# A hybrid mLSTM and sparse-attention trunk on one core: product lag in the attention backs, pieces of the gates' chain, and the order of the compression's weights

## The chip, the core and the metric

The kernel runs on one core of a Trainium2 chip. The metric is the device time of one execution in microseconds (us), as a median over several runs. Engines are named as in the profile: PE (TensorE matmuls), PEld (its weight loads), DVE (VectorE), ACT (ScalarE), POOL (GpSimd), SP (SyncE, which here only issues transfers).

## The reference

The model has 512 positions of width 1024 and two layers, each x += 1/2 SwiGLU, x += mixer, x += 1/2 SwiGLU, everything in float32. The first mixer is an mLSTM with 8 heads. The second is native sparse attention (NSA) with 16 query heads over 4 shared key/value heads, made once from the stream behind the first layer.

```python
log_i = ig + bif[0]; log_f = log_sigmoid(fg + bif[1])       # mLSTM gates
D = where(causal, b[t] - b[s] + log_i[s], -inf)             # b = cumsum(log_f)
h_out = (W @ v) / max(|den|, exp(-m));  W = exp(D - m) * (q @ k.T)
y = (rmsnorm(h_out, g_head) * sigmoid(og)) @ w_out
k_cmp = rmsnorm(silu((blocks(kc) + pe) @ w1) @ w2)          # compressed keys, v_cmp likewise
o = g_c * attn(q, k_cmp, v_cmp) + g_s * attn(q, k_sel, v_sel) + g_w * attn(q, k_win, v_win)
```

With 512 positions all eight blocks are selected and the window covers everything, so the selected and the window branch are both causal attention, each over its own keys and values.

## The kernel before

Activations lie transposed, features on partitions and the 512 positions along the free axis. Each float32 product is made of three float32r matmuls of a rounded high part and the remainder (`mm3`, L145): hi by hi, hi by lo, lo by hi. `split` (L151) makes the parts, the high one on ACT and the low one on DVE.

Weights come through one ring (`load_weight`, L102): SP issues a transfer of 512 KB into one of two `wraw` buffers, ACT rounds it into one of three `whi` and DVE makes `wlo`. The order of the weights is that in which the code asks for them, found in a dry pass, and a request loads up to two weights ahead.

The stages follow one another: ffn0, mlstm, ffn1, kv, ffn2, nsa, ffn3. In a stage Python generators write out the program order. `weave(main, fill, ratio)` takes one step of `main` and then on the average `ratio` steps of `fill`; a step of a projection is one `mm3`. Program order is not the order on an engine. The layer that places the instructions may put a later one first when it expects its operands sooner, with the earlier in program order preferred. An engine then works its own queue strictly in that order.

**mlstm (L311).** `project_qk(0)` takes eight steps, the row scale r is made, and `gates()` (L346) follows: a chain of about 25 operations on 8 partitions, most on DVE, with one exponential on ACT, to the running sums, the running maximum and its negative nM. All of it stands in one piece before the remaining 24 steps of `project_qk(0)`; the pair nM, the transposes of um and the columns uc and e2 stand behind 20 steps of `project_v(0)`. Later `heads(1)` is woven with `project_og(1)` and `project_out(0)` (64 steps, called rest) at 1.05, `finish(1)` (L517) with what is left at 4, and `project_out(1)` comes last. In `finish`, per head, a DVE operation scales num by a row that PE broadcasts, POOL multiplies by sig (L543), and `split` makes yhi and ylo, the operands of `project_out`.

**kv (L582)** makes the shared keys and values. `take` (L614) writes the unnormed keys and values A, with a shifted copy through POOL's DMA queue. `compress()` (L670) is returned as a generator and woven into ffn2, one step of it to 2.5 steps of ffn2 (L1000). Per kind (keys, values) and half it makes the operand F (A plus the block encoding, on POOL), splits it into Fh and Fl, waits three empty steps, and multiplies by two weights of c_w1, eight steps in all.

**nsa (L750).** A front per head makes scores S, row maxima on DVE, exponentials on ACT into pr, and the weighting by gate/z on POOL. A back per head (L880) has one PSUM accumulator po (one buffer for all heads): it starts with the product of the compressed weights ct (one buffer), and then works five groups. For each, PE transposes pieces of pr into one of two PSUM tiles pt, `split` makes pth and ptl (three buffers each), and the products of the group before are added to po, so products run one group behind. At the head's end ACT copies half of po and DVE adds the other into o. `compressed(b)` (L812) makes ct for a pair of heads; its last step waits until the back of head 2b-1 has begun, and the fronts of the pair stand behind it. `Steps` objects mix backs, fronts and fills (projections of later queries and half of the output) by the lines below, behind a start in which q1 takes four steps, then r, the gates, and the rest of q1 with fronts between.

```python
for _ in backs[h]:
    fill.steps(0.9)
    front.steps(2.5)
```

Of the kernel before, what the change touches and what calls it, by code (L numbers as in the profile page):

```python
# [10 lines left out]
F32 = mybir.dt.float32  # L11
F32R = mybir.dt.float32r
BF16 = mybir.dt.bfloat16
I32 = mybir.dt.int32
AF = mybir.ActivationFunctionType
ALU = mybir.AluOpType
# [29 lines left out]
def run(gen):  # L46
    for _ in gen:
        pass
# [42 lines left out]
class Net:  # L91
# [220 lines left out]
    def mlstm(self):  # L312
        nc, tc = self.nc, self.tc
        TT, STT, TS = nc.vector.tensor_tensor, nc.vector.scalar_tensor_tensor, nc.vector.tensor_scalar
        with ExitStack() as ctx:
# [32 lines left out]
            def gates():  # L348
                bif = self.g[:H, G_BIF:G_BIF + 2]
                li, f, t1, t2, t3 = (row(n, "big", BIG) for n in ("li", "f", "t1", "t2", "t3"))  # L350
                TT(li, pg[:H], r[:H], op=ALU.mult)
                TS(li, li, bif[:, 0:1], None, op0=ALU.add)
                TT(f, pg[32:32 + H], r[32:32 + H], op=ALU.mult)
                TS(f, f, bif[:, 1:2], None, op0=ALU.add)

                STT(t1, f, -1.0, f, op0=ALU.mult, op1=ALU.max)
                nc.scalar.activation(t1, t1, AF.Exp, scale=-1.0)
                TS(t2, t1, 2.0, None, op0=ALU.add)
                nc.vector.reciprocal(t3, t2)
                TT(t1, t1, t3, op=ALU.mult)  # L360
                TT(t2, t1, t1, op=ALU.mult)
                TS(t3, t2, 1.0 / 15.0, None, op0=ALU.mult)
                for c in (13.0, 11.0, 9.0, 7.0, 5.0, 3.0):
                    STT(t3, t3, 1.0 / c, t2, op0=ALU.add, op1=ALU.mult)
                STT(t3, t3, 1.0, t1, op0=ALU.add, op1=ALU.mult)
                TS(f, f, 0.0, None, op0=ALU.min)
                STT(f, t3, -2.0, f, op0=ALU.mult, op1=ALU.add)

                one = self.ones[:H, :1].to_broadcast([H, T])
                um = mp.tile([40, T], F32, name="um", tag="tmp", bufs=3)  # L370
                nc.gpsimd.memset(um, 0.0)
                nc.vector.tensor_tensor_scan(t1, one, f, 0.0, op0=ALU.mult, op1=ALU.add)
                TT(um[:H], li, t1, op=ALU.subtract)
                nc.vector.tensor_tensor_scan(t2, one, um[:H], 0.0, op0=ALU.mult, op1=ALU.max)
                TT(um[32:], t1, t2, op=ALU.add)
                TS(t2, t2, -1.0, None, op0=ALU.mult)
                yield
                nM = pair("nM", t2)
                up = ps_nm()[:, :160].rearrange("p (t c) -> p t c", t=NTB)
                for tb in range(NTB):  # L380
                    nc.tensor.transpose(up[:, tb, :], um[:, tb * P:(tb + 1) * P], self.ident[:40, :40])
                uc = mp.tile([P, NTB, H], F32, name="uc")
                nc.scalar.copy(uc, up[:, :, :H])
                e2 = mp.tile([P, NTB, H], F32, name="e2")
                nc.scalar.activation(e2, up[:, :, 32:], AF.Exp, scale=-2.0)
                yield nM, uc, e2
# [130 lines left out]
            def finish(half):  # L517
# [20 lines left out]
                for h in range(4 * half, 4 * half + 4):  # L538
                    pc = ps_nm()
                    self.mm(pc, pick(h), cr, True, True)  # L540
                    n = num[h]
                    STT(n, n, self.g[:, G_HEAD + h:G_HEAD + h + 1], pc, op0=ALU.mult, op1=ALU.mult)
                    nc.gpsimd.tensor_tensor(n, n, sig[h], op=ALU.mult)  # L543
                    hi = self.xp.tile([P, T], F32R, name="yhi", tag="xhi")
                    lo = self.xp.tile([P, T], F32R, name="ylo", tag="xlo")
                    self.split(n, hi, lo)
                    y[h] = (hi, lo)
                    yield
# [16 lines left out]
            g = gates()  # L565
            next(g)
            run(qk0)
            v0 = project_v(0)
            for _ in range(20):
                next(v0)  # L570
            nM, uc, e2 = next(g)
            run(v0)
# [11 lines left out]
            weave(heads(1), rest, 1.05)  # L584
            sigmoids(1)
            weave(finish(1), rest, 4)
# [4 lines left out]
    def kv(self):  # L591
# [17 lines left out]
        with ExitStack() as ctx:  # L609
            pp = ctx.enter_context(tc.tile_pool(name="kps", bufs=1, space=PSUM, reuse_waits="tile"))  # L610
            mp = ctx.enter_context(tc.tile_pool(name="ks", bufs=1, reuse_waits="tile"))
            ps_mm = lambda: pp.tile([P, T], F32, name="pmm", tag="mm", bufs=6)
            x, ssq = self.norm_in(G_KV)
            def take(b, ps):  # L614
                if b < 4:

                    for j in range(2):
                        t, s = A[b // 2][:, 2 * (b % 2) + j, :], slice(64 * j, 64 * j + 64)
                        TT(t[:64], ps[s], r[s], op=ALU.mult)
                        nc.gpsimd.dma_start(t[64:, :T - 1], t[:64, 1:])  # L620
                    return
                br = (b - 4) // 2
                sq = mp.tile([P, T], F32, name="ksq", tag="ksq", bufs=2)
                nc.scalar.activation(sq, ps, AF.Square)
                f = self.head_scale(mp, aux([P, NTB, 2]), sq, var, HD)
                fb = mp.tile([P, NTB, 2, HD], F32, name="kfb", tag="ksq", bufs=2)
                nc.scalar.activation(fb, f[:, :, :, None].to_broadcast([P, NTB, 2, HD]), AF.Copy, scale=HD ** 0.5)
                yield
                fp = aux([P, T])
                for tb in range(NTB):  # L630
                    self.mm(fp[:, tb * P:(tb + 1) * P], fb[:, tb].rearrange("p h d -> p (h d)"), self.ident, True, True)
                kn = mp.tile([P, T], F32, name="kn", tag="kn", bufs=2)
                nc.scalar.copy(kn, fp)
                STT(kn, ps, self.g[:, G_K + 1 + br:G_K + 2 + br], kn, op0=ALU.mult, op1=ALU.mult)
                for j in range(2):
                    K = self.K[2 * (b % 2) + j]
                    s, o = slice(64 * j, 64 * j + 64), slice(64 - 64 * j, 128 - 64 * j)
                    nc.scalar.activation(K[s, br, :], kn[s], AF.Copy)
                    TT(K[o, br, :], kn[s], K[s, br, :].bitcast(F32), op=ALU.subtract)

            held = []
            for b in range(8):
                w = self.weight("kv_t", b)
                ps = ps_mm()
                for k in range(KB):
                    self.mm3(ps, self.strip(w, k), x[k], k == 0, k == KB - 1)
                if b == 0:
                    rc, var = self.rstd_columns(ssq, aux([P, NTB]))
                if b == 1:
                    r = self.rstd_rows(rc, aux([P, T]))  # L650
                held.append(take(b, ps))
                if b > 0:
                    held = [t for t in held if next(t, t) is None]
            ps4 = [ps_mm() for _ in range(NTB)]
            for kp in range(4):
                w = self.weight("kv_v", kp)
                for tb in range(NTB):
                    for kk in range(2):
                        k = 2 * kp + kk
                        l = tuple(t[:, tb * P:(tb + 1) * P] for t in x[k])  # L660
                        self.mm3(ps4[tb], l, self.strip(w, kk), k == 0, k == KB - 1)
            for t in held:
                run(t)
            for tb in range(NTB):
                pv = ps4[tb].rearrange("p (h d) -> p h d", d=HD)
                V = self.V[tb]
                nc.scalar.activation(V[:, :, :HD], pv, AF.Copy, scale=rc[:, tb:tb + 1])
                STT(V[:, :, HD:], pv, rc[:, tb:tb + 1], V[:, :, :HD].bitcast(F32), op0=ALU.mult, op1=ALU.subtract)

        def compress():  # L670

            n = KVH * NCMP
            for kind in range(2):
                av = A[kind].rearrange("p h (c s) -> p s h c", s=16)
                hp = aux([P, 256])
                for half in range(2):
# [7 lines left out]
                    for _ in range(3):  # L684
                        yield
                    for j in range(2):
# [60 lines left out]
        return compress(), r  # L747


    def nsa(self):  # L750
        nc, tc = self.nc, self.tc
        TT, STT, TS = nc.vector.tensor_tensor, nc.vector.scalar_tensor_tensor, nc.vector.tensor_scalar
        with ExitStack() as ctx:
# [56 lines left out]
            def compressed(b):  # L810
# [25 lines left out]
                yield lambda: started[0] >= 2 * b  # L836
# [3 lines left out]
                t = cw[b] = mp.tile([P, T], F32R, name="ct", tag="ct", bufs=1)  # L840
# [4 lines left out]
            def head(h):  # L845
# [34 lines left out]
                def back():  # L880
# [3 lines left out]
                    held, left = None, [4, 4]  # L884
# [9 lines left out]
                    for group in groups:  # L894
# [10 lines left out]
                        if held:  # L905
                            apply(*held)
                        held = group, at, hi, lo
# [5 lines left out]
                    apply(*held)  # L913
# [52 lines left out]
            for _ in range(4):  # L966
                next(q1)
# [5 lines left out]
            for _ in q1:  # L973
                front.steps(1.2)
# [135 lines left out]
```

## Time and profile before

| | us |
|---|---|
| median of 3 runs (2060.71 to 2061.84) | 2061.43 |
| the profiled execution | 2058.35 |
| its span, first to last instruction | 2056.6 |
| PE busy in the span | 2024.7 |
| DVE, ACT, POOL busy | 1122.9, 817.0, 188.9 |

A wait is idle time of an engine before an instruction, put down to what ended it. A matmul's end is modelled, some 0.16 us behind the point at which the next one can start, so a PE wait as listed is a little shorter than what it costs.

### The profile page before, as it was taken

The page shows a single profiled execution, that of the slowest core. Times are in us where ns is not written, and L with a number is a line of the kernel's source. Part 1 is how long each engine was busy: PE and PEld are TensorE (multiplying, and loading weights), DVE is VectorE, ACT ScalarE, POOL GpSimd, SP SyncE. Part 2 cuts the span into 40 slices and gives each one's busy share as a digit, 9 for nine tenths or more (in the row PEclk, how much of TensorE's full clock was granted, in tenths as well). Part 3 has the DMA queues.
Part 4 walks back from the last instruction along what each step waited for, and adds up shares of the span by engine and source line. Part 5 has one row for each costly group of instructions (what it writes and reads, how often), then busy time and mean ns, then how long its engine had stood idle before and what let it go on. Part 6 is the DMA issues. An engine that isn't in the chain of part 4 may idle for free. (4 is left out here: it accounts for less than half of the span.)

```text
span 2056.6 us, 24443 instructions
## 1 busy us (share of the span) xinstructions
PE 2024.7 (98%) x9460; PEld 1662.0 (81%) x9460; DVE 1122.9 (55%) x1796; ACT 817.0 (40%) x1409; POOL 188.9 (9%) x235
## 2 busy tenths in 40 slices
PE   8999999999999999999999999999999999999999
PEld 6888888778878888888878888887777788888887
DVE  6434345777765444445656444445788874434443
ACT  5223233455643222223443322224888763223231
POOL 1000000012210000000101000001544420000000
PEclk9999999999999999999999999999999999999999
DMA  4232322323123322323333323333111113332332
GB/s 161 93 103 91 103 94 86 103 93 92 62 72 103 101 94 86 109 90 105 95 100 126 114 95 91 103 94 93 52 42 42 42 56 99 92 101 89 101 97 95
DMA packets 56468, 188.12 MB, mean 91 GB/s; under 512 B 6816, under 2 KB 7456, under 8 KB 56352
## 3 DMA queue, kind: packets, MB, share of 16 engines
q1 hardware_dynamic: 55392, 184.47, 28.8%
q8 instruction: 74, 1.21, 0.3%
q0 software_dynamic: 384, 1.05, 0.2%
q10 hardware_dynamic: 576, 1.05, 0.1%
q14 instruction: 42, 0.34, 0.1%
HBM read 177.10 MB, written 2.10 MB: 87 GB/s over the span
## 5 line engine op out<-in xcount | busy, mean ns | idle before, releaser
L124 ACT ACTIVATE whi<-wraw 128x1024 fp32r<-128x1024 f32 (+3 forms) x399 | 360.3, 916 | 989.5 <-PE pmm L143 813.3
L143 PE MATMUL pmm<-xhi,whi 128*128 128x512 f32 x1672 | 656.7, 393 | 7.6 <-ACT whi L124 7.6
L143 PE MATMUL pmm<-xhi,wlo 128*128 128x512 f32 x1672 | 653.6, 391 | 0.0
L143 PE MATMUL pmm<-xlo,whi 128*128 128x512 f32 x1672 | 653.0, 391 | 0.1
L125 DVE TENSOR_TENSOR wlo<-wraw,whi 128x1024 fp32r<-128x1024 f32 (+3 forms) x399 | 419.6, 1061 | 77.0 <-ACT whi L124 66.1
L143 PEld LDWEIGHTS pmm<-xhi,whi 128*128 128x128 f32 x1672 | 314.2, 188 | 70.4 <-ACT whi L124 8.8
L143 PEld LDWEIGHTS pmm<-xhi,wlo 128*128 128x128 f32 x1672 | 313.8, 188 | 66.9 <-DVE wlo L125 1.0
L143 PEld LDWEIGHTS pmm<-xlo,whi 128*128 128x128 f32 x1672 | 314.1, 188 | 62.4 <-DVE xlo L188 0.6
L143 PE MATMUL pmm<-ghi,whi 128*128 128x512 f32 x704 | 274.1, 389 | 0.0
L143 PE MATMUL pmm<-ghi,wlo 128*128 128x512 f32 x704 | 273.9, 389 | 0.0
L143 PE MATMUL pmm<-glo,whi 128*128 128x512 f32 x704 | 273.9, 389 | 0.0
L271 DVE TENSOR_TENSOR fu<-pmm,r 128x512 f32<-128x512 f32 x88 | 60.8, 691 | 259.0 <-PE pmm L143 258.9
L309 DVE SCALAR_TENSOR_TENSOR h<-pmm,h 128x512 f32<-128x512 f32 x96 | 66.1, 691 | 238.9 <-PE pmm L143 238.9
L269 DVE TENSOR_TENSOR ft<-pmm,r 128x512 f32<-128x512 f32 x88 | 60.8, 691 | 180.9 <-PE pmm L143 180.9
L143 PEld LDWEIGHTS pmm<-ghi,wlo 128*128 128x128 f32 x704 | 132.2, 188 | 27.6
L143 PEld LDWEIGHTS pmm<-ghi,whi 128*128 128x128 f32 x704 | 132.2, 188 | 27.3
L143 PEld LDWEIGHTS pmm<-glo,whi 128*128 128x128 f32 x704 | 132.2, 188 | 27.2
L198 POOL TENSOR_TENSOR ssq<-ssq,sq 128x512 f32<-128x512 f32 x18 | 28.0, 1556 | 999.6 <-ACT sq L197 999.6
L152 ACT ACTIVATE ghi<-ft 128x512 fp32r<-128x512 f32 x88 | 55.7, 633 | 79.1 <-DVE ft L272 79.1
L873 POOL TENSOR_SCALAR pr<-pr,rz,gate 128x512 f32<-128x512 f32 (+3 forms) x128 | 79.6, 631 | 77.8 <-DVE rz L869 68.3
L868 ACT ACTIVATE pr<-S,nx,c 128x512 f32<-128x512 f32 (+3 forms) x128 | 78.1, 617 | 0.9
L153 DVE TENSOR_TENSOR glo<-ft,ghi 128x512 fp32r<-128x512 f32 x88 | 60.4, 687 | 17.2 <-ACT ghi L152 17.1
(297 smaller groups left out, 2054.0 us busy)
## 6 DMA issues: line engine op xcount, KB each, us to landing
wraw<-in_ffn_in SPq DMA_DIRECT2D x176, 512.0 KB, 3.4
wraw<-in_ffn_out SPq DMA_DIRECT2D x64, 448.0 KB, 3.3
wraw<-in_ffn_out SPq DMA_DIRECT2D x32, 512.0 KB, 3.6
wraw<-in_m_qk SPq DMA_DIRECT2D x8, 512.0 KB, 3.4
wraw<-in_m_v SPq DMA_DIRECT2D x8, 512.0 KB, 3.5
wraw<-in_m_og SPq DMA_DIRECT2D x8, 512.0 KB, 3.4
wraw<-in_m_out SPq DMA_DIRECT2D x8, 512.0 KB, 3.4
wraw<-in_kv_t SPq DMA_DIRECT2D x8, 512.0 KB, 3.4
```

The lines of the kernel that those rows point to most:

```text
L124: nc.scalar.activation(hi[:p, c], raw[:p, c], AF.Copy)
L125: nc.vector.tensor_tensor(lo[:p, c], raw[:p, c], hi[:p, c].bitcast(F32), op=ALU.subtract)
L143: self.nc.tensor.matmul(out, lhsT, rhs, start=start, stop=stop)
L152: self.nc.scalar.activation(hi, src, AF.Copy)
L153: self.nc.vector.tensor_tensor(lo, src, hi.bitcast(F32), op=ALU.subtract)
L198: (nc.gpsimd if b < 4 else nc.vector).tensor_tensor(t, t, sq, op=ALU.add)
L269: nc.vector.tensor_tensor(t, pa, r, op=ALU.mult)
L271: nc.vector.tensor_tensor(u, pb, r, op=ALU.mult)
L309: nc.vector.scalar_tensor_tensor(h, po[j], 0.5, h, op0=ALU.mult, op1=ALU.add)
L868: nc.scalar.activation(s, S[:, i, :n], AF.Exp, bias=nx[:, i:i + 1], scale=cc, accum_out=z[:, i:i + 1])
L873: nc.gpsimd.tensor_scalar(s, s, rz[:, i:i + 1], gate[:, tb, gi:gi + 1], op0=ALU.mult, op1=ALU.mult)
```

## The change

The gates' chain yields eight times and is woven at 5 steps of qk and v to a piece, with nM, um's transposes, uc and e2 in the last piece. The multiply by sig goes to DVE in the second half. `heads(1)` takes 0.9 fill steps instead of 1.05, `finish(1)` 5 instead of 4. `compress()` starts before the `kv_v` projection: its first step (F, Fh and Fl of the keys' first half) stands there, one empty step follows instead of three, and elsewhere four stand in place of three; its first c_w1 weight comes before the first two of ffn2. In the attention, products run two groups behind, ct has two buffers and may be made one pair of heads earlier, and q1 takes all eight matmul steps before the row scale is made, with no front between.

```diff
 def gates():
     nc.scalar.activation(t1, t1, AF.Exp, scale=-1.0)
+    yield
...
+    yield
     for c in (13.0, 11.0, 9.0, 7.0, 5.0, 3.0):
         STT(t3, t3, 1.0 / c, t2, op0=ALU.add, op1=ALU.mult)
+        if c in (11.0, 7.0, 3.0):
+            yield
...
     yield
-    nM = pair("nM", t2)
+    gated.append(pair("nM", t2))
...
-    yield nM, uc, e2
+    gated.extend((uc, e2))
 def finish(half):
-    nc.gpsimd.tensor_tensor(n, n, sig[h], op=ALU.mult)
+    (nc.vector if half else nc.gpsimd).tensor_tensor(n, n, sig[h], op=ALU.mult)
...
-g = gates()
-next(g)
-run(qk0)
-v0 = project_v(0)
-for _ in range(20):
-    next(v0)
-nM, uc, e2 = next(g)
-run(v0)
+gated, rest = [], chain(qk0, project_v(0))
+weave(gates(), rest, 5)
+nM, uc, e2 = gated
+run(rest)
...
-weave(heads(1), rest, 1.05)
+weave(heads(1), rest, 0.9)
 sigmoids(1)
-weave(finish(1), rest, 4)
+weave(finish(1), rest, 5)
 def kv(self):
...
+    left = compress()
+    next(left)
     ps4 = [ps_mm() for _ in range(NTB)]
...
 def compress():
-    hp = aux([P, 256])
     for half in range(2):
...
-        for _ in range(3):
+        for _ in range(4 if half or kind else 1):
             yield
+        if half == 0:
+            hp = aux([P, 256])
...
-return compress(), r
+return left, r
 def nsa(self):
...
-    yield lambda: started[0] >= 2 * b
+    yield lambda: started[0] >= 2 * b - 2
-    t = cw[b] = mp.tile([P, T], F32R, name="ct", tag="ct", bufs=1)
+    t = cw[b] = mp.tile([P, T], F32R, name="ct", tag="ct", bufs=2)
...
-        if held:
-            apply(*held)
-        held = group, at, hi, lo
+        if len(held) == 2:
+            apply(*held.popleft())
+        held.append((group, at, hi, lo))
...
-    apply(*held)
+    while held:
+        apply(*held.popleft())
...
-for _ in range(4):
+for _ in range(KB):
     next(q1)
...
-for _ in q1:
-    front.steps(1.2)
+run(q1)
```

## Rows read from the trace of the kernel before

**Rows 1.** The page: busy time of the engines, and the commonest group of matmuls.

```profile
PE 2024.7 (98%) x9460; PEld 1662.0 (81%) x9460; DVE 1122.9 (55%) x1796; ACT 817.0 (40%) x1409; POOL 188.9 (9%) x235
...
L143 PE MATMUL pmm<-xhi,whi 128*128 128x512 f32 x1672 | 656.7, 393 | 7.6 <-ACT whi L124 7.6
```

**Rows 2.** Windows: stretch, its length, busy time of each engine, granted clock, DMA.

```profile
515.00:561.00 46.00, 45.91 (x218) 37.31 (x217) 38.93 (x68) 30.48 (x70) 11.24 (x12) 1.00 0.21 66
...
561.00:605.00 44.00, 39.31 (x170) 29.74 (x168) 31.55 (x57) 22.93 (x38) 10.07 (x7) 1.00 0.23 76
605.00:960.00 355.00, 355.00 (x1574) 294.18 (x1575) 161.24 (x201) 103.93 (x127) 4.55 (x3) 1.00 0.31 96
...
1424.00:1500.00 76.00, 71.74 (x422) 56.16 (x421) 53.44 (x150) 55.67 (x143) 33.22 (x46) 0.98 0.21 58
1500.00:1600.00 100.00, 95.86 (x599) 77.58 (x598) 81.39 (x215) 87.30 (x242) 50.31 (x74) 1.00 0.16 43
1600.00:1692.00 92.00, 90.65 (x510) 72.88 (x509) 71.95 (x144) 66.08 (x158) 31.38 (x45) 1.00 0.16 47
```

**Rows 3.** Waits of PE: who for whom, total us, times, longest us.

```profile
PE paux L143 <- ACT whi L124: 2.9, 2, 1.5
PE pmm L143 <- ACT yhi L152: 2.8, 2, 1.5
PE po L143 <- DVE ptl L153: 2.4, 3, 0.9
PE vps L143 <- DVE wlo L125: 1.7, 1, 1.7
PE po L143 <- DVE o L918: 1.4, 1, 1.4
PE pt L143 <- DVE rq L217: 1.4, 1, 1.4
PE po L143 <- ACT pth L152: 1.3, 5, 0.5
PE pt L900 <- DVE ct L153: 1.2, 2, 0.7
...
PE pmm L143 <- DVE ylo L153: 0.7, 1, 0.7
```

**Rows 4.** Timeline of the gates' chain: start, us, engine, line; then PE's first use.

```profile
391.08 3.34 DVE L359 RECIPROCAL t<-t 8x512 f32<-8x512 f32 x1
...
416.53 0.68 DVE L337 TENSOR_TENSOR nM<-t,nM 8x512 fp32r<-8x512 f32 x1 [0.16 <-ACT nM L336]
...
424.77 0.39 PE L143 MATMUL pnm<-nM,sel 128*128 128x512 f32 x1
```

**Rows 5.** Groups from 561 to 587 (finish of the second half), then the timeline of DVE.

```profile
L543 POOL TENSOR_TENSOR num<-num,sig 128x512 f32<-128x512 f32 x4 | 5.6, 1415 | 22.2 <-DVE num L542 22.2
...
L542 DVE SCALAR_TENSOR_TENSOR num<-num,gains,pnm 128x512 f32<-128x512 f32 x4 | 3.0, 738 | 0.7 <-PE pnm L143 0.7
...
577.43 1.61 DVE L153 TENSOR_TENSOR ylo<-num,yhi 128x512 fp32r<-128x512 f32 x1 [0.36 <-ACT yhi L152]
...
579.62 0.68 DVE L153 TENSOR_TENSOR ylo<-num,yhi 128x512 fp32r<-128x512 f32 x1
```

**Rows 6.** Timeline of POOL, SP (c_w1's issues) and PE around the end of kv.

```profile
985.91 2.39 POOL L679 TENSOR_TENSOR F<-A,gains 128x992 f32<-128x992 f32 x1
...
1032.44 0.33 SPq L117 DMA_DIRECT2D wraw<-in_c_w  x1
...
1056.62 0.33 SPq L117 DMA_DIRECT2D wraw<-in_c_w  x1
...
1062.50 0.38 PE L143 MATMUL paux<-whi,Fh 128*124 128x256 f32 x1 [1.55 <-ACT whi L124]
```

**Rows 7.** The longest wait of a product in NSA, and the window that follows it.

```profile
1485.59 0.50 PE L143 MATMUL po<-ct,VC 128*128 128x512 f32 x1 [1.43 <-DVE o L918]
...
1488.10:1491.40 3.30, 3.30 (x12) 2.84 (x11) 2.55 (x6) 1.06 (x1) 0.62 (x1) 0.50 0.00 0
```

More of the change, by code (lines that the diff above doesn't have):

```diff
@@ L367, in gates @@
                 STT(f, t3, -2.0, f, op0=ALU.mult, op1=ALU.add)
+                yield
                 one = self.ones[:H, :1].to_broadcast([H, T])
@@ L373, in gates @@
                 TT(um[:H], li, t1, op=ALU.subtract)
+                yield
                 nc.vector.tensor_tensor_scan(t2, one, um[:H], 0.0, op0=ALU.mult, op1=ALU.max)
@@ L608, in kv @@
         A = [lp.tile([P, KVH, T], F32, name=f"A{kind}") for kind in range(2)]
[L609 to L668, printed above, removed]
@@ L745, in compress, with take @@
             late.close()
-        return compress(), r
+        with ExitStack() as ctx:
+            pp = ctx.enter_context(tc.tile_pool(name="kps", bufs=1, space=PSUM, reuse_waits="tile"))
+            mp = ctx.enter_context(tc.tile_pool(name="ks", bufs=1, reuse_waits="tile"))
+            ps_mm = lambda: pp.tile([P, T], F32, name="pmm", tag="mm", bufs=6)
+            x, ssq = self.norm_in(G_KV)
+            def take(b, ps):
+                if b < 4:
+                    for j in range(2):
+                        t, s = A[b // 2][:, 2 * (b % 2) + j, :], slice(64 * j, 64 * j + 64)
+                        TT(t[:64], ps[s], r[s], op=ALU.mult)
+                        nc.gpsimd.dma_start(t[64:, :T - 1], t[:64, 1:])
+                    return
+                br = (b - 4) // 2
+                sq = mp.tile([P, T], F32, name="ksq", tag="ksq", bufs=2)
+                nc.scalar.activation(sq, ps, AF.Square)
+                f = self.head_scale(mp, aux([P, NTB, 2]), sq, var, HD)
+                fb = mp.tile([P, NTB, 2, HD], F32, name="kfb", tag="ksq", bufs=2)
+                nc.scalar.activation(fb, f[:, :, :, None].to_broadcast([P, NTB, 2, HD]), AF.Copy, scale=HD ** 0.5)
+                yield
+                fp = aux([P, T])
+                for tb in range(NTB):
+                    self.mm(fp[:, tb * P:(tb + 1) * P], fb[:, tb].rearrange("p h d -> p (h d)"), self.ident, True, True)
+                kn = mp.tile([P, T], F32, name="kn", tag="kn", bufs=2)
+                nc.scalar.copy(kn, fp)
+                STT(kn, ps, self.g[:, G_K + 1 + br:G_K + 2 + br], kn, op0=ALU.mult, op1=ALU.mult)
+                for j in range(2):
+                    K = self.K[2 * (b % 2) + j]
+                    s, o = slice(64 * j, 64 * j + 64), slice(64 - 64 * j, 128 - 64 * j)
+                    nc.scalar.activation(K[s, br, :], kn[s], AF.Copy)
+                    TT(K[o, br, :], kn[s], K[s, br, :].bitcast(F32), op=ALU.subtract)
+            held = []
+            for b in range(8):
+                w = self.weight("kv_t", b)
+                ps = ps_mm()
+                for k in range(KB):
+                    self.mm3(ps, self.strip(w, k), x[k], k == 0, k == KB - 1)
+                if b == 0:
+                    rc, var = self.rstd_columns(ssq, aux([P, NTB]))
+                if b == 1:
+                    r = self.rstd_rows(rc, aux([P, T]))
+                held.append(take(b, ps))
+                if b > 0:
+                    held = [t for t in held if next(t, t) is None]
+            left = compress()
+            next(left)
+            ps4 = [ps_mm() for _ in range(NTB)]
+            for kp in range(4):
+                w = self.weight("kv_v", kp)
+                for tb in range(NTB):
+                    for kk in range(2):
+                        k = 2 * kp + kk
+                        l = tuple(t[:, tb * P:(tb + 1) * P] for t in x[k])
+                        self.mm3(ps4[tb], l, self.strip(w, kk), k == 0, k == KB - 1)
+            for t in held:
+                run(t)
+            for tb in range(NTB):
+                pv = ps4[tb].rearrange("p (h d) -> p h d", d=HD)
+                V = self.V[tb]
+                nc.scalar.activation(V[:, :, :HD], pv, AF.Copy, scale=rc[:, tb:tb + 1])
+                STT(V[:, :, HD:], pv, rc[:, tb:tb + 1], V[:, :, :HD].bitcast(F32), op0=ALU.mult, op1=ALU.subtract)
@@ L883, in back @@
                     groups = (((0, 1), (0, 3)), ((0, 0),), ((0, 2), (1, 2)), ((1, 1), (1, 3)), ((1, 0),))
-                    held, left = None, [4, 4]
+                    held, left = deque(), [4, 4]
                     started[0] += 1
```

## The prediction

> **What bounds the kernel now.** I read the page first, for the busiest engine. PE is busy 2024.7 of 2056.6 us [rows 1], so only PE's gaps can be won; the other engines matter where they open one. The windows come next: they show where the gaps lie. From 605 to 960 us PE has none, and 1574 matmuls take 355 us, 0.2255 us each [rows 2]. So the large FFN stretches have nothing to give. From 561 to 605 PE misses 44 - 39.31 = 4.7 us, and in the three NSA windows 4.3 + 4.1 + 1.4 = 9.8 us [rows 2]. The list of PE's waits then says what ended each gap [rows 3]. The nine rows there add up to 15.8 us, and the change touches all nine. What they really cost is more, since a wait is counted from a matmul's modelled end: a matmul is listed with 0.393 us [rows 1] and the next starts after 0.2255, so each interruption costs about 0.16 us on top. Rows 3 hold 18 of them, 2.9 us. One gap has a sequel: after the 1.43 us wait at 1485.6 the granted clock is 0.50 for 3.3 us, which is the lower of the two levels, 1.2 GHz [rows 7]. Half of that time is lost, 1.7 us. Before the fall PE had that wait and a run of small score matmuls. All that the change can win by these rows is 15.8 + 2.9 + 1.7 = 20.4 us.
>
> **The change part by part.** The sum is made against the profiled execution, 2058.35 us (span 2056.6 and 1.75 around it); the median stands 3.1 us above it, and I add the same difference back.
>
> *Gates in pieces.* No operation is added or removed. Before, the whole chain stood ahead of the weights that come with the following steps, so on DVE's queue the weight split that PE needed came behind it; the longest single piece is a reciprocal of 3.34 us [rows 4]. PE stood 1.7 us for that split [rows 3]. In pieces, each weight split has its place ahead of the pieces written later. The chain itself then ends when? Its last piece stood behind 8 + 24 + 20 steps of qk and v, and now behind 8 + 8 x 5 = 48, so it is not due later. If it were, nM is complete at 417.2 and PE first uses it at 424.8 [rows 4], which covers 7.5 us. Gain 1.7 + 0.16 = 1.9 us; bounds from +0.5 (the reciprocal catches another split) to -1.9.
>
> *The end of mLSTM.* The steps left for `finish(1)` go from 64 - 47 = 17 to 64 - 40 = 24 (45 steps of `heads(1)` by 1.05 and by 0.9). Seven steps of three matmuls are 7 x 3 x 0.2255 = 4.7 us of PE work moved from the heads to the finish. Per head, DVE's scaling takes 0.74 us, POOL's multiply 1.42 on the average, and a low split 0.68, or 1.61 where it runs beside POOL [rows 5]. On DVE the multiply should be like the low split, 0.68 us: both read two 512-column operands of the same size. The chain per head gets about 0.7 us shorter and DVE's own part comes to 0.74 + 0.68 + 0.68 = 2.1 us per head. PE waited 2.8 + 0.7 us here [rows 3] in three gaps, 4.0 us in all. The new cover would hide most of it, but the work is taken from a stretch in which DVE is busy 38.9 of 46 us [rows 2]: with 4.7 us less of PE work in it DVE would need 38.9 of 41.3, less about a microsecond of weight splits that move along. There some of it comes back as PE waiting for DVE. I take 1.5 us of 4.0; bounds +1 to -4.
>
> The Trainium skill ("Perfetto Trace Analysis", Optimizing Scalar/DVE Operations) says that work moved between GpSimd and VectorE might not help, since they share an SBUF read port. By that rule the move gains nothing and the 1.5 us would be 0.8, from the cover alone (an estimate: half). The rows speak against it here, since the low split beside POOL loses 0.9 us, and with both operations on one engine there is nothing beside it.
>
> *kv into ffn2.* F was already made at 985.9 [rows 6], far ahead of its place in the program and 55 us before its use, so making it sooner is worth nothing. POOL's 2.39 us and the four transfers it issues stay where they are; the cost of the edit is 0, and if POOL were late the 55 us cover it. What matters is the weights' order: the first c_w1 transfer is issued at 1032.4 after two of ffn2 and now comes before them, and the second at 1056.6 is what PE waits for at 1062.5 [rows 6]. The two waits are 2.9 us [rows 3], 3.2 with the restarts. The first should go, but then ffn2's second weight comes one place later on SP, ACT and DVE, and its first matmuls alternate between two weights; some of it is given back. The second c_w1 weight still needs a buffer of the ring of three that the first one frees only after four steps. I take 1.7; bounds +1 to -3.2.
>
> *Start of NSA.* PE waits 1.4 us for the row scale [rows 3]. Four more steps of q1, 12 x 0.2255 = 2.7 us, now stand before it and cover it. The same 2.7 us are missing as filler beside the first fronts, where fills of q2 must stand in. Gain 1.6 less 0.7, 0.9; bounds +2 (all missing filler is idle, less 0.7) to -1.6.
>
> *Products two groups behind.* The same matmuls, transposes and splits. Products waited 1.3 + 2.4 us in eight gaps [rows 3], 3.7 + 8 x 0.16 = 5.0 us. One more group gives a split another round of fronts and fills before it is needed. ACT and DVE are busy 87.3 and 81.4 of 100 us in the middle window [rows 2], so they still run behind at times, and what is late next is a transpose that waits for one of two pt tiles. I take 2.8; bounds +8 to -5.0, the upper end from the second rival.
>
> *Compressed weights a pair ahead.* Transposes waited twice for ct's split, 1.2 us [rows 3], 1.5 with restarts. The split is still made once per pair and still holds a pt tile, but at a less loaded moment, and the even heads' fronts no longer stand behind it. I take half, 0.7; bounds +1.5 to -1.5.
>
> *The wait for o.* With its restart and the slow clock it cost 1.43 + 0.16 + 1.7 = 3.3 us, at one of 15 changes of head. The new order neither removes nor repeats it by design; I take half, 1.5; bounds +3.3 to -3.3.
>
> The sum: 1.9 + 1.5 + 1.7 + 0.9 + 2.8 + 0.7 + 1.5 = 11.0 us. 2058.35 - 11.0 = 2047.4, and by the median 2061.43 - 11.0 = **2050.4 us**.
>
> **The rivals.** *First, slower: the single accumulator.* Behind the last transposes of a head now stand the products of two groups instead of one, then ACT's copy and DVE's add, and the next head's first product needs the same po. If PE waits for that at most changes of head as it did once, 1.43 + 0.16 = 1.6 us [rows 7], it costs 1.6 each. The other terms without the wait for o are 9.5 us, so it decides from six changes on; at 12 of 15 it is 19.2 - 9.5 = 9.7 us slower, 2071. For it: one buffer for all heads. Against it: only one of 15 changes shows such a wait now, and the transposes of the next head are independent of po and can be placed before its first product. Chance 0.1.
>
> *Second, given back: two pt tiles.* The products no longer wait, but transposes run further ahead and wait for a pt tile, as they did twice for 0.6 us each [rows 3]. Once per head that is 16 x 0.6 = 9.6 us; the 11.0 us shrink to 1.4, and the time is 2060. For it: ACT at 87%. Against it: only two such waits now, and the number of transposes and splits is unchanged. A rule of the Trainium skill stands for this case ("Perfetto Trace Analysis", Optimization Strategy): a bubble that repeats can mean that there is no PSUM for the next tile, which a deeper lag with the same tiles doesn't mend. The few product waits are not regular in this trace, so I give it less than the forecast. Chance 0.12.
>
> *Third, the change does little.* The queues are not in program order: F at 985.9 shows it. If PE's order in NSA hardly changes, only the gates and kv remain, 1.9 + 1.7 = 3.6 us, 2057.8. Chance 0.08.
>
> **How the numbers follow.** Forecast 0.70, rivals 0.10, 0.12 and 0.08. About 0.2% or 4 us is what a measurement can tell from no change. The second and third rival lie within it, 0.20; the first beyond it, 0.10; the forecast's own range, 2043 to 2057, is faster, 0.70. The range for 8 in 10 reaches from 2042, where nearly all of the 20.4 us are won, to 2060, which takes in the second and third rival.
>
> **What would show it.** Right: PE's waits lose the rows for wlo at vps, yhi and rq, and po's waits for pth and ptl fall below 1.5 us together; PE's idle time from 1424 on falls below 6 us, and the span to about 2046. The multiply by sig at L543 shows about 0.7 us on DVE. Wrong: PE waits of po for o at many heads, of pt for ptl or ct once per head, or a new wait in the heads from 515 on for Wh or Wl; a second stretch at clock 0.50; or the old waits under other names.

## Result and profile after

The change makes the kernel slower: 2079.24 us (median of 4 runs, 2076.91 to 2080.89) against 2061.07 (4 runs, 2060.49 to 2061.84), a ratio of 1.0087 with the interval 1.0070 to 1.0105. The profiled execution took 2079.09 us with a span of 2077.3, so the span grew by 20.7. That is 2.5 us more than the medians differ, since the profiled execution before, 2058.35 us, lies under its median.

The page's first part, of the kernel after:

```profile
PE 2035.3 (98%) x9460; PEld 1664.0 (80%) x9460; DVE 1125.6 (54%) x1800; ACT 816.8 (39%) x1409; POOL 184.5 (9%) x231
```

PE is busy 10.6 us longer than in [rows 1], and idle 42.0 us instead of 31.9. To find the place I took the same event in both traces (a first or last instruction of a kind) and compared the times between them:

| stage | after less before, us |
|---|---|
| up to the first value projection | +0.45 |
| from there to the first use of nM (24.39 to 26.64) | +2.25 |
| `heads(1)` | -1.0 |
| `finish(1)` (43.32 to 44.37) | +1.05 |
| kv: last V to the last product of the compression (113.41 to 111.42) | -2.0 |
| NSA (267.45 to 287.16) | +19.7 |

The sum is 20.45 of 20.7, and nearly all of it is NSA. The windows of NSA after answer to those in [rows 2], with the three stretches at the lower clock between them (stretch, length, busy time of PE, PEld, DVE, ACT, POOL, granted clock, DMA):

```profile
1424.00:1500.00 76.00, 68.05 (x377) 51.13 (x375) 49.78 (x143) 50.27 (x131) 31.13 (x44) 0.93 0.19 54
1455.00:1458.30 3.30, 3.30 (x9) 1.65 (x8) 2.12 (x5) 3.30 (x14) 0.67 (x1) 0.50 0.00 0
1472.10:1478.80 6.70, 5.63 (x21) 4.14 (x22) 2.55 (x7) 4.38 (x12) 3.05 (x5) 0.50 0.23 81
1500.00:1600.00 100.00, 90.11 (x544) 71.29 (x544) 75.62 (x185) 76.80 (x205) 44.81 (x64) 0.98 0.16 43
1502.80:1506.10 3.30, 3.30 (x15) 2.79 (x14) 1.90 (x4) 1.85 (x4) 0.77 (x1) 0.50 0.38 144
1600.00:1714.00 114.00, 109.98 (x619) 87.17 (x618) 88.26 (x186) 83.62 (x206) 39.13 (x56) 1.00 0.13 42
```

PE now misses 8.0 us of the first 76 where [rows 2] has 4.3, and 9.9 of the next 100 where it has 4.1. PE's waits after, to be read beside [rows 3], say who ended these gaps (who for whom, total us, times, longest; those of pt, S and po are in NSA):

```profile
PE pt L846 <- POOL cp L842: 10.9, 8, 2.2
...
PE pt L907 <- DVE ptl L153: 3.4, 4, 2.1
PE pnm L387 <- DVE um L381: 2.7, 1, 2.7
PE S L143 <- ACT pr L875: 2.2, 5, 1.6
PE dm L143 <- ACT th L152: 1.8, 2, 1.4
PE po L143 <- DVE ptl L153: 1.4, 2, 1.0
PE po L143 <- ACT pth L152: 1.4, 2, 0.7
...
PE paux L143 <- DVE wlo L125: 0.8, 1, 0.8
...
PE po L143 <- DVE o L926: 0.5, 2, 0.3
```

More than half of NSA's waits is one that did not exist: the transposes of the compressed weights (pt<-cst,cp) stand 10.9 us for cp, in eight gaps. The waits that the change aimed at did shrink: po for ptl and pth from 3.7 to 2.8 us, ct's 1.2, o's 1.4 and rq's 1.4 to 0.5 in all. But NSA's waits grew from 9.0 to 20.6 us. Of the 19.7 us, 11.6 are these waits. About another 5.0 are the lower clock: 13.3 us of it in the windows above against 3.3 in [rows 7], half of the difference lost. The last 3 us I have not taken apart; eight more restarts at 0.16 us, the prediction's price, would be 1.3 of them (an estimate).

**How the new wait comes about.** The timeline of one pair, after (start, us, engine, line and operation, and in brackets the idle time before it with its releaser):

```profile
1494.80 0.28 PE L143 MATMUL S<-cmpb,identb 128*128 128x256 bf16 x1
...
1495.12 0.42 DVE L832 TENSOR_REDUCE cnx<-S 128x8 f32<-128x256 f32 x1 [1.14 <-PE S L143]
...
1496.26 0.41 DVE L835 TENSOR_TENSOR cp<-S,cnx 128x256 f32<-128x256 f32 x1
...
1496.76 0.62 POOL L836 TENSOR_TENSOR cp<-cp,c 128x256 f32<-128x256 f32 x1 [0.16 <-DVE cp L835]
...
1498.02 0.41 DVE L838 TENSOR_REDUCE cz<-cp 128x8 f32<-128x256 f32 x1
...
1498.68 0.40 PE L143 MATMUL pmm<-xhi,wlo 128*128 128x512 f32 x1
...
1499.57 0.17 DVE L841 TENSOR_TENSOR crz<-crz,gate 128x8 f32<-128x8 f32 x1
...
1499.88 0.62 POOL L842 TENSOR_TENSOR cp<-cp,crz 128x256 f32<-128x256 f32 x1 [2.51 <-DVE crz L841]
...
1500.56 0.63 PE L846 MATMUL pt<-cst,cp 128*64 128x128 f32 x4 [1.48 <-POOL cp L842]
```

From the last matmul of the compressed scores (the mask, at 1494.80) to cp lie ten small operations on DVE, ACT and POOL, which take 5.7 us until L842 ends at 1500.50. PE's queue held only 4.3 us of work behind that matmul, up to 1499.08, and then had the transposes, so it stood. POOL is named as releaser, but it is not what is slow: it was itself idle 2.51 us for DVE's crz. The same pair before:

```profile
1487.88 0.28 PE L143 MATMUL S<-cmpb,identb 128*128 128x256 bf16 x1
...
1495.40 0.62 POOL L835 TENSOR_TENSOR cp<-cp,crz 128x256 f32<-128x256 f32 x1 [4.49 <-DVE crz L834]
...
1497.31 0.60 PE L839 MATMUL pt<-cst,cp 128*64 128x128 f32 x4
```

There the chain took longer, 8.1 us until 1496.02, yet nobody waited: the late gate had put 9.4 us of other work between the scores and the transposes in PE's queue. (3.3 us of that work ran at the lower clock [rows 7].) The other pairs show the same. Measured in that way in the timelines, the seven pairs that the gate moves, the second to the eighth, have

| kernel | chain to cp, us (mean) | PE's work before the transposes, us (mean) |
|---|---|---|
| before | 4.9 to 8.1 (6.5) | 6.8 to 13.0 (10.3) |
| after | 4.6 to 8.2 (6.4) | 4.3 to 6.5 (5.2) |

The chain did not get longer, the work that covers it was halved, and at each of the seven pairs PE waits for the difference. The kernel before already stood close to such waits: at its second pair the transposes begin within 0.1 us of cp's end.

### The profile page after: what moved, and what is told of

The parts are those of the page before. It is cut to its first block, busy times and chain, and to the rows that moved or that the text cites. A ratio compares the mean times of both kernels' runs of the same rounds, so it can differ in the third digit from the quotient of the medians.

```text
span 2077.3 us, 24423 instructions
## 1 busy us (share of the span) xinstructions
PE 2035.3 (98%) x9460; PEld 1664.0 (80%) x9460; DVE 1125.6 (54%) x1800; ACT 816.8 (39%) x1409; POOL 184.5 (9%) x231
## 3 DMA queue, kind: packets, MB, share of 16 engines
q0 software_dynamic: 384, 1.05, 0.2%
q10 hardware_dynamic: 576, 1.05, 0.1%
## 4 chain that ended last, share of the span: by engine, by line
PE 87%; DVE 6%; ACT 4%; issue 1%; POOL 1%; DMA 0%; SPq 0%; ACTq 0%; DVEq 0%; POOLq 0%
PE pmm L143 79%; PE S L143 2%; ACT pr L875 1%; DVE wlo L125 1%; PE pt L907 1%; PE po L143 1%; PE vps L143 1%; PE paux L143 1%; PE pn L143 1%; ACT whi L124 1%; ACT pth L152 1%; DVE rq L220 0%; DVE ptl L153 0%; DVE nx L871 0%; PE dm L143 0%
## 5 line engine op out<-in xcount | busy, mean ns | idle before, releaser
L124 ACT ACTIVATE whi<-wraw 128x1024 fp32r<-128x1024 f32 (+2 forms) x399 | 360.0, 916 | 993.9 <-PE pmm L143 819.2
L143 PE MATMUL pmm<-xhi,whi 128*128 128x512 f32 (+1 forms) x1672 | 657.2, 393 | 7.4 <-ACT whi L124 7.3
L143 PE MATMUL pmm<-xhi,wlo 128*128 128x512 f32 (+1 forms) x1672 | 653.4, 391 | 0.3 <-DVE wlo L125 0.2
L143 PE MATMUL pmm<-xlo,whi 128*128 128x512 f32 (+1 forms) x1672 | 653.1, 391 | 0.0
L125 DVE TENSOR_TENSOR wlo<-wraw,whi 128x1024 fp32r<-128x1024 f32 (+2 forms) x399 | 419.2, 1060 | 77.7 <-ACT whi L124 66.6
L143 PEld LDWEIGHTS pmm<-xhi,whi 128*128 128x128 f32 (+1 forms) x1672 | 314.1, 188 | 70.8 <-ACT whi L124 9.0
L143 PEld LDWEIGHTS pmm<-xhi,wlo 128*128 128x128 f32 (+1 forms) x1672 | 313.7, 188 | 67.8 <-DVE wlo L125 2.0
L143 PEld LDWEIGHTS pmm<-xlo,whi 128*128 128x128 f32 (+1 forms) x1672 | 314.0, 188 | 62.6 <-DVE xlo L188 0.3
```

The lines of the kernel that those rows point to most:

```text
L124: nc.scalar.activation(hi[:p, c], raw[:p, c], AF.Copy)
L125: nc.vector.tensor_tensor(lo[:p, c], raw[:p, c], hi[:p, c].bitcast(F32), op=ALU.subtract)
L143: self.nc.tensor.matmul(out, lhsT, rhs, start=start, stop=stop)
```

## Experiments

Each ratio is to the kernel before, run on the same chip; its medians there were 2059.19 to 2059.77 us, so 0.001 of a ratio is 2.06 us. Letters in the expectations are theories: A puts the loss on the early compressed weights (A1 and A2 are two readings of it), the others on other parts of the change.

**One part of the change taken back: u_ct, u_lag, u_q1, u_gates.** Edits against the kernel after:

```diff
# u_ct
-yield lambda: started[0] >= 2 * b - 2
+yield lambda: started[0] >= 2 * b
-name="ct", tag="ct", bufs=2
+name="ct", tag="ct", bufs=1
# u_lag
-if len(held) == 2:
-    apply(*held.popleft())
-held.append((group, at, hi, lo))
+if held:
+    apply(*held)
+held = group, at, hi, lo
...
# u_q1
-for _ in range(KB):
+for _ in range(4):
     next(q1)
-run(q1)
+for _ in q1:
+    front.steps(1.2)
# u_gates (and the chain without the new yields)
...
-weave(gates(), rest, 5)
+g = gates(); next(g); run(qk0)
+v0 = project_v(0)
+for _ in range(20): next(v0)
+nM, uc, e2 = next(g)
```

> The changed kernel with one part undone: the compressed weights are again made only when the back of head 2b-1 has begun, in one ct buffer. Theory A (the early compressed weights cost the time: PE transposes cp too soon and waits 10.9 us in 8 gaps for POOL's multiply, and the slow clock follows): 12 to 18 us faster than the changed kernel, about 2061 to 2067, and no wait of pt for cp. Theory B (the lag of two costs it): less than 4 us faster. Theory C (q1 without fronts at the start costs it): less than 4 us faster.

> The changed kernel with the products again one group behind their transposes. Theory A: within 4 us of the changed kernel's 2079, the waits for cp stay. Theory B: 8 to 16 us faster, and PE's waits of pt for ptl (3.4 us) and S for pr (2.2 us) go. Theory C: within 4 us.

> The changed kernel with q1 split again: four steps before the row scale, the rest with fronts between. The first product of the attention came 4.0 us later against the start of the stage; theory C: those 4 us come back, 4 to 6 faster than the changed kernel. Theories A and B: the start was late because the first cp was waited for, so less than 3 us faster.

> The changed kernel with the gates' chain again in one piece. The stretch from the first value projection to the first use of nM grew by 2.25 us, with a wait of 2.7 us of PE for um and a slow clock behind it. If the pieces cause it: 2 to 3 us faster than the changed kernel, and the old wait of 1.7 us for wlo is back in its place. Rival: the wait comes from elsewhere (no difference).

| kernel | median us (runs) | ratio to before, interval |
|---|---|---|
| u_ct | 2062.67 (11) | 1.0013, 1.0004 to 1.0022 |
| u_lag | 2087.92 (4) | 1.0134, 1.0120 to 1.0148 |
| u_q1 | 2078.31 (5) | 1.0086, 1.0073 to 1.0100 |
| u_gates | 2077.16 (4) | 1.0083, 1.0069 to 1.0096 |

Taking back the early weights returns 0.0074, 15 us of the 18. What is left of the change without them, u_ct, is still 0.0013, 2.7 us, slower than before. Taking back the lag makes it 0.0047, 10 us, worse, which none of the theories expected: with the early weights the lag of two helps. The other two can't be told from the kernel after. PE's waits of u_ct in NSA:

```profile
PE pt L907 <- DVE ptl L153: 3.7, 5, 1.7
PE pt L846 <- POOL cp L842: 3.2, 2, 2.2
```

cp is waited for twice instead of eight times, and the clock is 1.00 in all three of its windows of NSA. Of the 3.2 us left, 2.2 are the first pair's, with a chain of 11.0 us; in u_q1, which gives q1 its fronts back, that pair has a chain of 6.9 us and no wait. The other 1.0 is the second pair's. In u_q1 cp has 9.1 us in 7 gaps and rq its 1.4 us again: the moved steps traded one wait for the other.

**One part alone on the kernel before: e_lag, e_ct, ct_gate.** e_lag is the lag of two, e_ct the early gate with two ct buffers, ct_gate the early gate with the one buffer of before:

```diff
# e_ct and ct_gate
-yield lambda: started[0] >= 2 * b
+yield lambda: started[0] >= 2 * b - 2
# e_ct only
-name="ct", tag="ct", bufs=1
+name="ct", tag="ct", bufs=2
```

> The kernel before with one part of the change: products two groups behind. If the lag helps as it did with the early compressed weights (undoing it there cost 9 us): 3 to 6 us faster than before, the waits of po for pth and ptl (3.7 us) nearly gone. If it only moves the wait to the transposes' two tiles: within 2 us of before, with waits of pt for ptl of 3 to 4 us. If it is harmful by itself: over 2 us slower.

> The kernel before with one part of the change: compressed weights one pair ahead, two ct buffers. Theory A (they alone cost the time): 15 to 26 us slower than before, with waits of pt for cp of 10 us and more. Theory B (they cost only together with the lag or the q1 start): less than 5 us slower.

> The kernel before with the compressed weights' gate one pair earlier, ct still in one buffer. If the gate alone does the harm: 15 us or more slower than before, as with both (26.5). If the second buffer is what lets it happen (with one, ct's split waits for the pair before anyway and the order stays): less than 8 us slower.

Measured: e_lag 2060.70 us (11 runs), 1.0005, 0.9996 to 1.0015; e_ct 2085.83 (4), 1.0129, 1.0115 to 1.0144; ct_gate 2101.22 (4), 1.0208, 1.0194 to 1.0222. PE's waits in NSA, first e_ct:

```profile
PE pt L839 <- POOL cp L835: 11.2, 6, 2.7
PE po L143 <- ACT pth L152: 4.6, 15, 0.7
PE po L143 <- DVE ptl L153: 4.5, 7, 2.1
```

Then ct_gate:

```profile
PE pt L839 <- POOL cp L835: 9.5, 7, 2.3
PE po L143 <- ACT pth L152: 6.7, 18, 0.7
PE pt L900 <- DVE ptl L153: 6.5, 12, 1.1
PE S L143 <- ACT pr L868: 4.4, 10, 1.3
```

The gate alone costs 43 us, and with the second buffer 27: the gate is the culprit, and the buffer softens it. Beside the cp waits others grow: po's for pth and ptl from 3.7 to 9.1 us in e_ct, and in ct_gate po's for pth, the transposes' for a pt tile and the scores' for pr. In ct_gate two windows of 6.8 us stand at a granted clock of 0.52 and 0.50 (stretch, length, busy times, clock, DMA):

```profile
1532.00:1538.80 6.80, 5.88 (x21) 3.74 (x19) 2.29 (x5) 2.82 (x7) 0.77 (x1) 0.52 0.14 55
1583.00:1589.80 6.80, 6.59 (x24) 4.99 (x24) 3.68 (x18) 4.36 (x15) 2.13 (x3) 0.50 0.04 13
```

The lag alone wins nothing. PE's waits of e_lag in NSA show where its gain went:

```profile
PE pt L900 <- DVE ptl L153: 3.8, 5, 1.6
...
PE po L143 <- DVE ptl L153: 1.2, 2, 1.0
```

po's waits for ptl and pth fall from 3.7 [rows 3] to 1.2 us, and the transposes wait 3.8 us for a pt tile instead: the second rival's mechanism. The rule that the prediction set beside that rival (the Trainium skill, "Perfetto Trace Analysis", Optimization Strategy: a repeating bubble can mean too little PSUM for the next tile) agrees with this row, five waits for a tile in sixteen heads.

**A third pt tile: e_lag_pt.** e_lag with the tile taken from the scores:

```diff
-name="S", tag="S", bufs=5
+name="S", tag="S", bufs=4
...
-name="pt", tag="pt", bufs=2
+name="pt", tag="pt", bufs=3
```

> The kernel before with products two groups behind, and three PSUM tiles pt for the transposes in place of two (four for scores and projections in place of five). If the two pt tiles are what takes the lag's gain away (waits of pt for ptl, 3.8 us): those waits go below 1 us, and the time is 2 to 5 us under before unless scores now wait for their tiles. If not: within 1 us of the lag alone, 2060 to 2061.

Measured: 2065.19 us (7 runs), 1.0029, 1.0018 to 1.0039, slower than the 2060 to 2061 of the lag alone. PE's waits in NSA, from the fastest of the seven runs (2062.70 us):

```profile
PE po L143 <- DVE ptl L153: 4.6, 7, 2.1
...
PE S L143 <- ACT qs L780: 1.2, 1, 1.2
PE pmm L143 <- ACT pr L868: 1.1, 1, 1.1
PE S L143 <- ACT pr L868: 1.1, 4, 0.4
```

No transpose waits for a pt tile any more, the splits are late again, and the scores wait for the tile that they lost. The wait goes round between the tiles.

**Distance, with the early gate kept: x_space, x_late.** x_space is the kernel after with five empty steps of the fronts between the chain and the gate. x_late takes the gate and the transposes out of the fronts, and puts the transposes of the next pair at a fixed place in the products' own order:

```diff
# x_space
+for _ in range(5):
+    yield lambda: True
 yield lambda: started[0] >= 2 * b - 2
# x_late
-yield lambda: started[0] >= 2 * b - 2
-pt = ps_t()
...
 held.append((group, at, hi, lo))
+if j == 1 and group is groups[2] and b + 1 in cps:
+    transposed(b + 1)
```

> The changed kernel with five empty steps of the fronts between cp's last operation and its transposes, the gate as early as in the change. Theory A1 (PE's transposes stand too soon behind the chain that makes cp, nothing covers its 5 to 6 us): the waits for cp go and it is 12 us or more faster than the changed kernel, as with the late gate. Theory A2 (what hurts is that the even heads' fronts run earlier and crowd ACT and DVE): less than half of that.

> The changed kernel with cp's transposes and split taken out of the fronts and put behind the third group of the head before the pair; the fronts have no gate there at all. Theory A1: at least as fast as with the late gate, 2063 or less, no wait for cp. Theory A2 (the early fronts hurt): still 2070 or more.

Measured: x_space 2065.54 us (7 runs), 1.0029, 1.0017 to 1.0040; x_late 2065.98 (5), 1.0033, 1.0020 to 1.0046. PE's waits of x_space in NSA:

```profile
PE pt L848 <- POOL cp L842: 4.5, 5, 2.1
```

and of x_late:

```profile
PE pt L911 <- DVE ptl L153: 6.0, 7, 2.3
PE pt L848 <- POOL cp L842: 2.2, 1, 2.2
```

Distance alone, with the gate as early as in the change, brings back 0.0058 of the 0.0087, 12 us. It is thus not the early place of ct or its second buffer that costs, but how closely the transposes follow their scores. Little distance was enough: over the same seven pairs PE's work before the transposes is 5.8 us in the mean instead of 5.2 and the chain 6.1 instead of 6.4, so the cp waits did not go, as A1 had it, but fell from 10.9 to 4.5 us. The rest of the gain lies in NSA's other waits, 7.5 us instead of 9.7, and in the clock, which falls once instead of three times. x_late removes all cp waits but the first pair's and gets no further, 3 us short of A1's 2063: there the transposes take a pt tile in the midst of a head, and those of the products wait 6.0 us for one. But it speaks against A2, that the even heads' fronts hurt by running early: here no gate holds them at all, and the time is not the 2070 or more that A2 asks.

**The parts outside NSA: k_kv, m_mul, m_fin, g_three, best1.** All against the kernel before: k_kv is the kv part of the change; m_mul the multiply by sig on DVE in the second half; m_fin that with the weaving ratios 0.9 and 5; g_three the gates in pieces, woven at 3 steps to a piece instead of 5; best1 is k_kv, m_mul and g_three together.

```diff
# k_kv (with compress() moved ahead and its empty steps, as in the change)
+left = compress()
+next(left)
 ps4 = [ps_mm() for _ in range(NTB)]
# m_mul
-nc.gpsimd.tensor_tensor(n, n, sig[h], op=ALU.mult)
+(nc.vector if half else nc.gpsimd).tensor_tensor(n, n, sig[h], op=ALU.mult)
# m_fin: m_mul and
-weave(heads(1), rest, 1.05)
+weave(heads(1), rest, 0.9)
-weave(finish(1), rest, 4)
+weave(finish(1), rest, 5)
# g_three: the change's gates() with
+weave(gates(), rest, 3)
```

> The kernel before with the kv part alone (compress started before the value projection, first c_w1 weight ahead of ffn2's). In the changed kernel the stretch from the last V to the end of the compression was 2.0 us shorter. If that is this part's doing: 1.5 to 2.5 us faster than before, PE's waits of paux for whi (2.9 us) gone. Rival: the 2 us depended on where the stage began (no difference).

> The kernel before with the multiply by sig on DVE in the second half, ratios as before. If the multiply's place is what made yhi and ylo late (3.5 us of waits): 1.5 to 3 us faster. If DVE then is as late as POOL was: within 1 us.

> The kernel before with the multiply on DVE and the two ratios of the change (0.9 and 5). In the changed kernel the two stretches together came out equal to before, with new waits in the heads (dm for th 1.8 us, pn for Wl 0.4 us). If the ratios take from the heads what they give the finish: 1 to 3 us slower than with the multiply alone. If the cover counts: 1 us or more faster than with the multiply alone.

> The kernel before with the gates' chain in the pieces of the change, but woven at 3 steps of qk and v to a piece instead of 5. If PE's transposes of um were late because the chain was stretched over 40 steps: the wait for um falls below 0.5 us, the wait of vps for wlo (1.7 us) is gone too, and the stretch to the first use of nM is 1 to 2 us shorter than before. If pieces as such delay the chain: the wait for um stays at over 1.5 us.

> The kernel before with the kv part, the gates in pieces at 3 steps, and the multiply on DVE; ratios, lag, q1 and compressed weights as before. Sum of the stretches: 1.7 + 1.5 + 0.4 = 3.6 us faster than before, 2055 to 2057. If the kv gain is undone in the attention by slow clocks as in the run of it alone: within 2 us of before.

| kernel | median us (runs) | ratio to before, interval |
|---|---|---|
| k_kv | 2059.53 (11) | 1.0001, 0.9992 to 1.0010 |
| m_mul | 2060.25 (11) | 1.0005, 0.9997 to 1.0014 |
| m_fin | 2059.55 (11) | 1.0007, 0.9998 to 1.0016 |
| g_three | 2060.37 (11) | 1.0006, 0.9998 to 1.0015 |
| best1 | 2060.08 (11) | 1.0004, 0.9995 to 1.0013 |

None can be told from no change. Each removes the wait that it aims at, in the profiled run, and shows another. The gates: DVE's part of the chain's end in the kernel after, around the transposes of um,

```profile
415.76 0.65 DVE L125 TENSOR_TENSOR wlo<-wraw,whi 128x512 fp32r<-128x512 f32 x1
416.45 0.68 DVE L381 TENSOR_TENSOR um<-t,t 8x512 f32<-8x512 f32 x1
```

and PE's wait of g_three for the same um, where the pieces are written sooner:

```profile
PE pnm L387 <- DVE um L381: 2.5, 1, 2.5
```

Before, PE waited 1.7 us for wlo [rows 3]. In pieces the split comes first and um later, and PE waits for um, 2.7 us after and 2.5 in g_three. For m_mul, a wait of PE:

```profile
PE pnm L143 <- DVE num L542: 0.8, 1, 0.8
```

yhi's 2.8 us [rows 3] are gone, and a wait for num has come; `finish(1)` takes 42.94 us instead of 43.32. In k_kv the stretch of the compression is 1.7 us shorter, as predicted, but the profiled run has a fall of the clock at 1431.9 and another at 1599.2, and its NSA is 2.3 us longer (stretch, length, busy times, clock, DMA):

```profile
1431.90:1435.20 3.30, 3.30 (x13) 2.31 (x12) 1.40 (x9) 0.59 (x1) 0.00 (x0) 0.50 0.43 97
1599.20:1602.50 3.30, 3.30 (x11) 2.72 (x11) 1.78 (x6) 3.30 (x11) 1.44 (x3) 0.50 0.13 47
```

**An attempt to beat both: best2.** best1 with all eight steps of q1 first, and one fill step after each front step of head 0 to make up for the filler that went with them:

```diff
 if not front.step():
     assert fill.step()
+elif h == 0:
+    fill.step()
```

> As the one before, and q1 takes its eight steps before the row scale, with one fill step after each front step of the first head, so that the first cp is not waited for. If the missing filler was what made the start of the attention late: 1 to 2 us faster than the one before, no wait of pt for rq and none over 0.5 us for the first cp. If not: slower by 1 to 4 us.

Measured: 2078.19 us (4 runs), 1.0091, 1.0076 to 1.0107. The first cp wait is 1.3 us instead of 2.2, but PE now waits 11.9 us for ptl in 9 gaps and 4.8 for pr in 11. That the fills taken early are missing later is likely, but was not tried by itself. No kernel tried here beats the kernel before.

## Why the prediction was wrong

It said 2050.4 us, 11.0 less than before, with 2060 as the upper end; the change costs 18.

**Compressed weights a pair ahead: -0.7 with bounds of 1.5 on either side; it is +15 in the change (u_ct), +27 alone (e_ct).** This is the step that failed. The prediction took from the trace what the operation itself waits for, ct's split and a pt tile, and said the moment would be "less loaded". It did not ask what the transposes read. cp is the end of a chain of ten small operations on three engines, and the trace of before shows no wait for it, because 6.8 to 13.0 us of PE's queue covered it. The late gate looked like a constraint and was the spacing. The chain of 4.9 to 8.1 us at the seven pairs that the gate moves was there to read in the trace of before; how much of the cover would go was not. Measured after, the seven pairs wait 8.8 us, six times the bound, and the first pair's 2.2 us come from the start of NSA (below). That distance is the cause is shown by x_space, which adds nothing but empty steps; they also hold back the fronts behind them, but in x_late those fronts run without a gate, and its ratio is the same within the intervals (1.0033 against 1.0029). The knock-on part (more waits for pth, ptl and pr, and the lower clock) goes away with it in u_ct, but was not separated from it.

**Products two groups behind: -2.8; it is 0 alone (e_lag), about -10 beside the early weights (u_lag).** The mechanism of the gain was right: po's waits fell. What was late next is what the prediction named, a pt tile, but it gave this a chance of 0.12; the lag alone ended so, within 2 us of before. e_lag_pt shows that the scores have no tile to spare.

**The wait for o and the slow clock: -1.5.** The one long wait for o went, 1.4 to 0.5 us in all, but the clock in NSA fell three times instead of once: 5.0 us more lost (an estimate: half of 10.0 us) instead of up to 1.7 won.

**Gates: -1.9; the stage is +2.25.** The wait for wlo went, as predicted. The cover named, 7.5 us to nM's first use, was true of nM and not of the piece that holds it: the same last piece has um's transposes, which stand in PE's queue among the value projection's matmuls, and these wait 2.7 us. That is 1.0 us more than the wait for wlo. Right behind it, from 417.2 to 420.5, the granted clock is 0.51, which is enough for the rest. u_gates, with the gates in one piece, has wlo's 1.7 us again, no wait for um and a clock of 1.00 there, but its median is not clearly better.

**End of mLSTM: -1.5; about 0.** The sizes of the operations were right. The groups from 563 to 590 after (busy us, mean ns, idle before):

```profile
L549 DVE TENSOR_TENSOR num<-num,sig 128x512 f32<-128x512 f32 x4 | 2.7, 685 | 0.0
L153 DVE TENSOR_TENSOR ylo<-num,yhi 128x512 fp32r<-128x512 f32 x4 | 2.7, 684 | 0.0
```

The multiply takes 0.685 us, and no low split is held up to 1.61 us as in [rows 5]. The heads also lost their seven steps: PE has 225 matmuls there instead of 246. But `heads(1)` got only 1.0 us shorter for 4.7 us less of work, and `finish(1)` only 1.05 longer with it. The cover hid most of the 4.0 us, and the heads gave nearly all of it back, where the prediction kept 1.5: dm's 1.8 us for th in the list of waits above are in `heads(1)`. m_mul alone is 1.0005: the rule of the Trainium skill ("Perfetto Trace Analysis", Optimizing Scalar/DVE Operations), that moving work between GpSimd and VectorE might not help, holds for the time, though not for the durations, which did get shorter.

**kv into ffn2: -1.7; the stage is -2.0.** Right: c_w1's first transfer is issued at 1022.4, ten us sooner than in [rows 6], the 2.9 us of waits are gone and 0.8 for wlo came. In the median it is lost (k_kv 1.0001).

**Start of NSA: -0.9; about 0.** rq's wait is gone, and the fronts that lost their place beside q1 make the first cp late by 2.2 us. The prediction named the missing filler but not the chain that it covered, as above.

**The rivals.** The first, po as the single accumulator, did not come: o is waited for 0.5 us in all. The second came, in part, as shown. None of the three had the mechanism that decided. Of the prediction's own signs of being wrong two came: three stretches at 0.50, and waits under other names (cp, um, th). All four forecasts moved within waits that the trace of before lists; the loss came from one that it doesn't list.

## What to carry to other kernels

Before a gate, a lag or an order is loosened, follow the moved instruction's operands back to their chain, and measure in the old trace how much work stands in the in-order queue between the start of that chain and its consumer: that distance is cover, and no list of waits shows it. Here, with PE 98% busy, a wait removed mostly showed the next one (wlo and um, ptl and pt, rq and cp), so a part's row in the list of waits does not say what the part is worth. Test parts alone before they are added: here all the other parts together came to 1.0013, no gain at all, and one part with a forecast of 0.7 us decided.

## What was not expected of the hardware

The granted clock does not answer to one short wait in the same way each time. The 1.42 us wait of pt for rq is in the profiled runs of before, m_fin, g_three, u_q1 and ct_gate with the clock at 1.00 behind it, and in those of e_lag, e_ct, k_kv, m_mul and best1 with 3.3 us at about 0.50, the lower level, 1.2 GHz, that begin about half a microsecond behind its end or sooner. Kernels with more waits in NSA mostly have more such falls there: one with 9.0 us of waits before, three with 20.6 after, five to seven with 25 to 31 in e_ct, u_lag and ct_gate, each for 3.3 or some 6.8 us; but u_ct and e_lag_pt have none with 12 to 13. Half the length of a fall is lost, 1.7 us of 3.3, which is more than the 1.42 us wait ahead of it.
